# A second level of seven products in the MLP's second layer

## The chip, the cores and the metric

The kernel runs on one core of a Trainium2 chip. The metric is the time of one execution on the device in microseconds. A second number, the span, comes from one execution that the hardware profiler recorded: from its first to its last instruction.

The core has five engines, each with its own queue that it works through in order: TensorE (PE in the profile; loading its stationary operand is listed apart as PEld), VectorE (DVE), ScalarE (ACT), GpSimd (POOL) and SyncE (SP), which here issues nearly all DMA transfers. Matmuls write to PSUM, which has eight banks of 512 fp32 columns; all other operands lie in SBUF; DRAM is reached by DMA.

## The reference

One layer of a diffusion backbone over 256 context tokens and 2048 latent tokens, with a model width of 1024. The part at issue is the MLP at its end:

```
def sq_relu_mlp(h, w1, w2):
    return jnp.square(jax.nn.relu(h @ w1)) @ w2
...
        h = rms_norm(xp, norm2_g[l]) * (1 + sc2) + sh2
        xp = xp + g2 * sq_relu_mlp(h, w1[l], w2[l])
...
        h = rms_norm(xs, norm2_g[l]) * (1 + sc2) + sh2
        xs = xs + g2 * sq_relu_mlp(h, w1[l], w2[l])
```

`w1` is 1024 x 4096, `w2` 4096 x 1024. The second layer multiplies the 2304 x 4096 activations by `w2`, scales by the gate `g2` (one per column, a different one for context and latent tokens), and adds the residual `x`.

## The kernel before

Every fp32 matrix product is done as three fp32r matmuls: each operand is split into a high part (a copy rounded to fp32r, on ScalarE) and a low part (the operand minus its high part, on VectorE, both inputs in SBUF), and `mm3` (lines 86 to 88) issues high x high, low x high or high x low into the same PSUM accumulation.

The stages follow each other: input projection, Fourier mixing and attention (to about 1325 us), output projection and norm, MLP layer one (`w1`, about 1590 to 2273 us), and MLP layer two (`w2`), which the change rewrites. Layer one (lines 1542 to 1544 issue its matmuls) works in 48 steps `q` of seven items `p`; VectorE splits weights there (line 1268) and forms sums of them (line 1514), GpSimd forms sums of its results (`g_add`, lines 1584 to 1590), and `g_stores` (line 1596) writes them to DRAM as `sop[p][b]`, 128 x 16 x 384 each.

Both layers use a scheme of seven products for eight, in the form with 15 additions. For layer two the tokens are halved (`NTH` = 9 tiles of 128 tokens in each half), the 4096 inputs are halved (16 chunks `k` of 128), and the 1024 outputs are halved (512 columns). Each of the seven products is 9 token tiles x 16 chunks x 512 columns, over left operands `sop[p]` (sums of activations, made in layer one) and right operands that are quarters of `w2` or their sums. Three of these sums are made during layer one by `ts_load` and `ts_sum` and put in DRAM as `tsum[k]`; the fourth is a difference of two loads (line 1221).

Layer two runs the products in the order `PO = (1, 2, 6, 7, 5, 3, 4)`. For each product `i` there are three blocks `b` of three token tiles, and for each block 16 chunks `k`; per chunk and tile one `mm3`, 128x128 by 128x512. Three PSUM banks of a block fill side by side; six buffers in all let the next block start while the last is read.

What feeds it:

- `t_load(n)` loads one chunk of the right operand (256 KB) through `raw` (line 1180), a ring of eight; `t_prep(n)` splits it (lines 1223 and 1224) into one of 22 buffers (`OPB` = 9 shared with layer one, `16 + AHEAD - OPB` of its own). A product's 16 chunks stay in SBUF for its three blocks. `PREP` lays down by hand between which matmuls each is split.
- `s_load(m)` loads four chunks of three tiles of the left operand (768 KB, line 1193, a ring of three under the tag `hr`); `s_prep(m)` splits two chunks at a time (128x768, lines 1236 and 1237).
- `y_post` takes a finished product out of PSUM. Running sums `UU` (nine tiles) and `U3` (nine tiles) stay in SBUF for the whole stage. Products 2, 5, 3 and 4 each complete one of the four quarters of the result (`target`): VectorE adds or subtracts the running sum (lines 1765 and 1767), multiplies by the gate (1772) and adds the residual (1773), which `x_load` (line 1748) fetched from `xnew`; `y_store` (line 1779) sends it out.

GpSimd has no work in this stage. Under `manual_schedule` the instructions stand on each engine's queue in exactly the order in which the loops emit them, and SP issues transfers in that order too, waiting where a buffer is not yet free. `mk_gate` forms the gate `g2` during the first product. At the very end the last product's three tiles are finished one after the other so that only one is left after the last matmul (lines 1830 and 1838 to 1844). The first loads and splits of layer two are emitted at the end of layer one (lines 1713 to 1724).

Of the kernel before, what the change touches and what calls it, by code (L numbers as in the profile page):

```python
# [36 lines left out]
def f32(ap):  # L37
    return ap.bitcast(F32)


def body(tc, a, out):
    nc = tc.nc
    ctx = ExitStack()
    with ctx:
# [21 lines left out]
        tsum = [scratch(f"tsum{k}", [P, 3, 512]) for k in range(16)]  # L66
# [1132 lines left out]
        OPB, AHEAD = 9, 6  # L1199
        PO = (1, 2, 6, 7, 5, 3, 4)  # L1200
        w2s = a["w2"][0].rearrange("(n k p) o -> p n k o", p=P, k=16)
        TR, TO, SR, SO, own = {}, {}, {}, {}, {}

        def op(nm, shared=True):
            if shared:
                return [ms2.tile([P, 512], F32R, tag=f"op{x}", name=f"op{x}{nm}", bufs=OPB) for x in "hl"]
            return [own["wk"].tile([P, 512], F32R, tag=f"t{x}", name=f"t{x}{nm}", bufs=16 + AHEAD - OPB) for x in "hl"]

        def t_load(n):

            p, k = PO[n // 16], n % 16
            TR[n] = []
            for rc in {1: (11,), 2: (21,), 3: (22,), 5: (0,), 7: (1,), 6: (2,), 4: (2, 21)}[p]:
                r, c = divmod(rc, 10)
                src = w2s[:, r - 1, k, (c - 1) * 512:c * 512] if r else tsum[k][:, c]
                TR[n].append(raw(f"b{rc}_{n}", src))

        def t_prep(n):
            src, *more = TR.pop(n)
            for t in more:  # L1220
                nc.vector.tensor_sub(src, src, t)
            hi, lo = op(f"T{n}", n % (16 + AHEAD) < OPB)
            nc.scalar.copy(hi, src)
            nc.vector.tensor_sub(lo, src, f32(hi))
            TO[n] = hi, lo

        def s_load(m):
            i, r = divmod(m, 12)
            b, c = divmod(r, 4)
            SR[m] = hr_load(f"sr{m}", sop[PO[i]][b][:, 4 * c:4 * c + 4, :])  # L1230

        def s_prep(m):
            src = SR[m // 2][:, m % 2 * 2:m % 2 * 2 + 2, :]
            pool, bufs = (ms2s, 2) if m % 3 < 2 else (own["t6"], 1)
            hi, lo = (pool.tile([P, 2, 384], F32R, tag=f"s{x}", name=f"s{x}{m}", bufs=bufs) for x in "hl")
            nc.scalar.copy(hi, src)  # L1236
            nc.vector.tensor_sub(lo, src, f32(hi))  # L1237
            SO[m] = hi, lo

# [260 lines left out]
        with c5r, ExitStack() as c5:  # L1502
# [155 lines left out]
            with tc.manual_schedule():  # L1658
                for n, (q, p) in enumerate(ITEMS):
# [42 lines left out]
                    if q - 1 in TSETS and p == 7:  # L1702
                        k = TSETS.index(q - 1)
                        nc.sync.dma_start(tsum[k], TS.pop(k))
# [8 lines left out]
                    if q == NQ - 1 and p == 7:  # L1713
                        s_load(0)
                        for n in range(4):
                            t_load(n)
                        s_load(1)
                    if q == NQ - 1 and p == 4:
                        t_prep(0)
                        s_prep(0)  # L1720
                        for n in (1, 2):
                            t_prep(n)
                squares()
                s_prep(1)
# [7 lines left out]
        with ExitStack() as c6:  # L1732
            wk = own["wk"] = c6.enter_context(tc.tile_pool(name="y_w", bufs=2, reuse_waits="tile"))
            t6 = own["t6"] = c6.enter_context(tc.tile_pool(name="y_t", bufs=2, reuse_waits="tile"))
            pp = c6.enter_context(tc.tile_pool(name="y_p", bufs=2, space=PSUM, reuse_waits="tile"))
            g2 = [wk.tile([P, D], F32, tag=f"g2_{s}", name=f"g2_{s}", bufs=1) for s in range(2)]
            UU, U3, X, ST = {}, {}, {}, []

            def target(p, t):

                return {2: (t, 0), 5: (t + NTH, 1), 3: (t, 1), 4: (t + NTH, 0)}.get(p)

            def x_load(i, b):
                for j in range(3):
                    tg = target(PO[i], 3 * b + j)
                    if tg:
                        X[j] = t6.tile([P, 512], F32, tag="x", name=f"x{i}_{b}_{j}", bufs=4)
# [168 lines left out]
```

## Time and profile before

| | before |
|---|---|
| median of 3 runs | 2979.64 us (2975.64 to 2981.17) |
| span of the profiled execution | 2975.5 us |
| MLP layer two, first to last start of a matmul | 2273.4 to 2970.4 us |
| last 5 us | VectorE on the last tile, its store |
| granted TensorE clock, mean | 0.995 |

Times in rows of the profile are microseconds from the start of the span unless they are marked ns. A row of a group gives the line, engine and operation, the tiles (output, then inputs), the shape, the count, the busy time in us and the mean in ns of one, and then the engine's idle time just before these instructions. A row of a stretch gives, for the interval, its length, then each engine's busy time with its count of instructions in the order PE, PEld, DVE, ACT, POOL, then the granted TensorE clock, the mean share of the 16 DMA engines, and GB/s. A row of single instructions gives start and duration, engine, line, operation, tiles and shape. A matmul's duration overlaps the next one's start, so what it costs is the distance between starts.

### The profile page before, as it was taken

Reading aid. Unit: us, or ns where it says so; the run is one execution under the profiler, and the core shown is the slowest. Engines: PE = TensorE matmul, PEld = TensorE weight load, DVE = VectorE, ACT = ScalarE, POOL = GpSimd, SP = SyncE. Lnnn points to the kernel's source line nnn. Section 1 sums busy time; section 2 is a strip of 40 time slices with the busy share of each in tenths; the row PEclk is TensorE's granted clock in tenths of the full one; section 3 lists DMA queues with packets and bytes.
Section 4 is the critical chain, followed back from the end, with each engine's and each line's share of the span. In section 5 each row is a group of like instructions: output and inputs, shape, how many; then the busy total and the mean of one; then the engine's idle time right before and its main releaser. Section 6 shows DMA issues by size and latency. Waiting matters only on the chain.

```text
span 2975.5 us, 43868 instructions
## 1 busy us (share of the span) xinstructions
PE 2914.6 (98%) x15481; PEld 2512.7 (84%) x15481; DVE 2025.9 (68%) x3379; ACT 1580.1 (53%) x3540; POOL 1022.5 (34%) x839
## 2 busy tenths in 40 slices
PE   8999999999999999999999999999999999999999
PEld 5888887778888888878888999999999888888887
DVE  6666775789888888865458778777776344344554
ACT  4333322688888889964346556556555322232221
POOL 1111112178888988851222333333332000000000
PEclk9999999999999999999999999999999999999999
DMA  7777878512120121215686677676666454445563
GB/s 274 204 195 205 226 195 250 193 52 76 42 110 28 70 84 35 86 58 157 202 251 215 218 239 226 219 238 214 221 200 228 145 171 162 138 145 174 195 215 106
DMA packets 394413, 495.58 MB, mean 167 GB/s; under 512 B 26403, under 2 KB 307056, under 8 KB 391122
## 3 DMA queue, kind: packets, MB, share of 16 engines
q1 hardware_dynamic: 386560, 477.63, 50.4%
q0 software_dynamic: 2992, 7.28, 0.8%
q10 hardware_dynamic: 4642, 7.88, 0.8%
q8 instruction: 122, 2.00, 0.3%
q14 instruction: 97, 0.79, 0.1%
HBM read 315.20 MB, written 179.57 MB: 166 GB/s over the span
## 4 chain that ended last, share of the span: by engine, by line
PE 90%; DVE 3%; ACT 2%; DMA 2%; issue 1%; POOL 1%; SPq 0%; ACTq 0%; DVEq 0%; POOLq 0%
PE Ss L920 10%; PE ps L86 8%; PE ps L87 8%; PE ps L88 8%; PE pj L86 4%; PE pj L88 4%; PE pj L87 4%; PE pts L976 4%; PE po L88 4%; PE po L86 4%; PE po L87 4%; PE pA L1542 2%; PE pA L1543 2%; PE pB L1542 2%; PE pA L1544 2%; PE pC L1544 2%
## 5 line engine op out<-in xcount | busy, mean ns | idle before, releaser
L925 DVE TENSOR_REDUCE mxs<-Ss 128x1 f32<-128x512 f32 x640 | 421.8, 687 | 80.4 <-PE Ss L920 69.9
L1237 DVE TENSOR_TENSOR sl<-sr,sh 128x768 fp32r<-128x768 f32 x168 | 161.7, 963 | 339.9 <-ACT sh L1236 339.4
L967 POOL TENSOR_TENSOR P0s<-P0s,P1s 128x1024 f32<-128x1024 f32 x124 | 365.3, 2946 | 10.3
L1236 ACT CAST sh<-sr 128x768 fp32r<-128x768 f32 x168 | 140.2, 835 | 424.9 <-PE ps L87 424.9
L1584 POOL TENSOR_TENSOR gs<-g,g 128x384 f32<-128x384 f32 x48 | 70.2, 1464 | 483.3 <-ACT g L1554 392.3
L944 ACT ACTIVATE P1s<-Ss,mxs 128x512 f32<-128x512 f32 x320 | 217.3, 694 | 35.6 <-DVE mxs L928 33.4
L86 PE MATMUL pj<-wh,hh 128*128 128x512 f32 x576 | 229.6, 399 | 0.7 <-ACT fo L374 0.7
L87 PE MATMUL ps<-tlT,sh 128*128 128x512 f32 x585 | 229.3, 392 | 0.0
L86 PE MATMUL ps<-thT,sh 128*128 128x512 f32 x585 | 229.2, 392 | 0.0
L87 PE MATMUL pj<-wl,hh 128*128 128x512 f32 x576 | 227.5, 395 | 0.5 <-DVE wl L496 0.5
L88 PE MATMUL ps<-thT,sl 128*128 128x512 f32 x585 | 227.7, 389 | 0.0
L88 PE MATMUL pj<-wh,hl 128*128 128x512 f32 x576 | 226.4, 394 | 0.0
L944 ACT ACTIVATE P0s<-Ss,mxs 128x512 f32<-128x512 f32 x320 | 215.8, 696 | 6.5 <-DVE mxs L928 6.3
L920 PE MATMUL Ss<-KS0s,Qs 128*128 128x512 f32 x640 | 201.8, 424 | 16.9 <-ACT P1s L944 15.6
L920 PE MATMUL Ss<-KS1s,Qs 128*128 128x512 f32 x640 | 210.9, 434 | 4.8 <-ACT P0s L944 4.0
L976 PEld LDWEIGHTS pts<-ident,P0s 128*128 128x128 f32 x1280 | 159.1, 141 | 45.4 <-ACT ahs L982 2.8
L976 PE MATMUL pts<-ident,P0s 128*128 128x128 f32 x1280 | 191.7, 273 | 3.4 <-DVE als L987 1.8
L1553 ACT ACTIVATE g<-uz 128x384 f32<-128x384 f32 x144 | 75.8, 527 | 207.3 <-DVE uz L1576 180.7
L982 ACT CAST ahs<-pts 128x512 fp32r<-128x512 f32 x256 | 151.3, 593 | 47.9 <-PE pts L976 39.7
L987 DVE TENSOR_TENSOR als<-pts,ahs 128x512 fp32r<-128x512 f32 x256 | 165.8, 681 | 11.5 <-ACT ahs L982 11.5
L966 POOL TENSOR_SCALAR P1s<-P1s,tots 128x1024 f32<-128x1024 f32 x124 | 166.8, 1346 | 5.6
L86 PE MATMUL ps<-ophT,sh 128*128 128x512 f32 x423 | 165.9, 392 | 1.1 <-DVE uz L1576 1.1
(615 smaller groups left out, 8248.2 us busy)
## 6 DMA issues: line engine op xcount, KB each, us to landing
sr<-sd SPq DMA_DIRECT2D x84, 768.0 KB, 4.4
a<-in_w SPq DMA_DIRECT2D x184, 256.0 KB, 4.0
sd<-gs SPq DMA_DIRECT2D x192, 192.0 KB, 1.9
sd<-g SPq DMA_DIRECT2D x144, 192.0 KB, 4.0
wm<-in_w_mod SPq DMA_DIRECT2D x32, 512.0 KB, 4.9
Qs<-qd SPq DMA_DIRECT2D x32, 512.0 KB, 3.5
b<-in_w SPq DMA_DIRECT2D x64, 256.0 KB, 4.9
b<-tsum SPq DMA_DIRECT2D x64, 256.0 KB, 4.6
```

The source lines that it names most:

```text
L86: nc.tensor.matmul(ps, lh, rh, start=first, stop=False)
L87: nc.tensor.matmul(ps, lh, rl, start=False, stop=False)
L88: nc.tensor.matmul(ps, ll, rh, start=False, stop=last)
L920: nc.tensor.matmul(S[:, :w], self.Q[:, x, m, j * P:j * P + P], self.hd.KS[m][:, b * 512:b * 512 + w], start=(x == 0), stop=(x == 1))
L925: nc.vector.tensor_reduce(self.mx[j][:, m, b:b + 1], self.S[j, m, b], axis=AX.X, op=ALU.max)
L944: nc.scalar.activation(dst, S, AF.Exp, bias=self.mx[j][:, m, 6:7], accum_out=self.sm[j][:, m, b:b + 1])
L966: nc.gpsimd.tensor_scalar(p, p, tot[:, 3:4], 0.0, op0=ALU.mult, op1=ALU.add)
L967: nc.gpsimd.tensor_add(d, d, p)
L976: nc.tensor.transpose(pt[:, c:c + P], self.p0[j][:, (kb + t) * P:(kb + t + 1) * P], ident)
L982: nc.scalar.copy(t, self.pt[kb])
L987: nc.vector.tensor_sub(t, self.pt[kb], f32(self.A[kb][0]))
L1237: nc.vector.tensor_sub(lo, src, f32(hi))
```

## The change

Layer two is rewritten; layer one keeps its work, except that two of its sums `tsum[k]` now share one DRAM tensor. The order `PO` of the seven outer products stays.

Within each outer product, eight of its nine token tiles are computed with the same scheme once more. The tiles form 2 rows of 4, the 16 chunks form 2 halves of 8, the 512 columns 2 halves of 256. So there are seven inner products `x` in the order 1, 5, 6, 7, 2, 3, 4, of 4 tiles x 8 chunks x 256 columns. The ninth tile is computed directly, in four further pieces (`"p"`) that use right operands which the inner products have anyway, and one extra split (`x = 0`). That gives 32 slots of 24 matmuls of 128x128 by 128x256.

- The left operands of inner products 5, 6, 7 and 3 are sums that GpSimd forms from loaded tiles (`s_sum`, 128x1024); the loads (`r_load`) fetch 8 chunks of one tile, 512 KB in pieces of 512 bytes, and some are fetched twice. ScalarE and VectorE then split each operand of a slot (`s_split`), through a ring of four buffers.
- The right operands are loaded as four quadrants and combined by `t_sum`: for inner products 5 and 6 on VectorE, for 7 and 4 on GpSimd (128x512, two chunks of 256 columns). Each is split (`t_split`) through a ring of 11.
- `v_copy` and `u2_add` take the inner running sums out of PSUM; later inner products accumulate onto banks A, B and C directly. There is one buffer for each of seven banks.
- The outer running sums no longer stay in SBUF. They are DRAM tensors `uu` and `ut`, in nine pieces of 128x512. For each piece of each product `z_load` fetches the sums and the residual, `z_pre` (GpSimd) adds the inner sum, `z_eva` (VectorE, from PSUM) adds the product, `z_mul` (VectorE) multiplies by the gate or stores the sum back to DRAM, `z_out` (GpSimd, and VectorE for the last four pieces) adds the residual and stores the result.
- All of it is put in order by times counted in slots: `at(i, t, fn, ...)` emits an action before slot `t` of product `i`.

The core of the diff:

```diff
-        tsum = [scratch(f"tsum{k}", [P, 3, 512]) for k in range(16)]
+        tsum = [scratch(f"tsum{k}", [P, 2, 3, 512]) for k in range(8)]
+        uu, u3 = ([scratch(f"{x}{n}", [P, 512]) for n in range(9)] for x in ("uu", "ut"))
...
+        TX, SX = (1, 0, 5, 6, 7, 2, 3, 4), (1, 5, 6, 7, 2, 3, 4)
+        QUAD = {"b11": (0, 0), "b12": (0, 1), "b22": (1, 1), "b21": (1, 0)}
...
+        def t_load(i, quad, u):
+            rc, *more = {1: (11,), 2: (21,), 3: (22,), 5: (0,), 7: (1,), 6: (2,), 4: (2, 21)}[PO[i]]
+            nm = f"{quad}_{i}_{u}"
+            if quad in ("b11", "b12"):
+                t = raw(nm, t_src(rc, quad, u))
+            else:
+                t = own["t6"].tile([P, 512], F32, tag="rb", name=nm, bufs=8)
+                nc.sync.dma_start(t.rearrange("p (k f) -> p k f", f=256), t_src(rc, quad, u))
+            TR[i, quad, u] = t
+            for m in more:
+                x = own["t6"].tile([P, 512], F32, tag="rx", name=f"x{nm}", bufs=1)
+                nc.sync.dma_start(x.rearrange("p (k f) -> p k f", f=256), t_src(m, quad, u))
+                nc.vector.tensor_sub(t, t, x)
...
+        def t_split(i, x, u):
+            src = TR[i, {1: "b11", 0: "b12", 5: "b11", 6: "b11", 7: "b12", 2: "b21", 3: "b22", 4: "b11"}[x], u]
+            n = (i * 8 + TX.index(x)) * 4 + u
+            hi, lo = op(f"T{i}_{x}_{u}", n % TRING < OPB)
             nc.scalar.copy(hi, src)
             nc.vector.tensor_sub(lo, src, f32(hi))
...
+            TO[i, x, u] = hi, lo
...
+            last = n % 4 == 3
+            hi, lo = (own["wk" if last else "ys"].tile([P, 1024], F32R, tag=f"s{x}", name=f"so{x}{n}", bufs=1 if last else 3) for x in "hl")
             nc.scalar.copy(hi, src)
             nc.vector.tensor_sub(lo, src, f32(hi))
...
+            SO[key] = [[t[:, k * P:k * P + P] for k in range(8)] for t in (hi, lo)]
...
+            RROLE = {(0, 0): "r0", (0, 1): "r0", (1, 0): "r1", (1, 1): "r2"}
+            def r_load(i, r, c, j, role=None):
+                role = role or RROLE[r, c]
+                t = t6.tile([P, 1024], F32, tag=role, name=f"{role}_{i}_{r}{c}{j}", bufs=4)
+                nc.sync.dma_start(t.rearrange("p (k t) -> p k t", t=P), s_src(i, r, c, j))
+                RQ[i, role, j] = t
...
+            def s_sum(i, x, j):
+                r0, r1, r2 = (RQ.get((i, f"r{n}", j)) for n in range(3))
+                if x == 5:
+                    nc.gpsimd.tensor_add(r1, r1, r2)
+                elif x == 6:
+                    nc.gpsimd.tensor_sub(r1, r1, r0)
+                elif x == 7:
+                    nc.gpsimd.tensor_sub(r2, r0, r2)
+                else:
+                    nc.gpsimd.tensor_sub(r1, r0, r1)
...
+            def t_sum(i, x, u):
+                b11, b12, b22, b21 = (TR.get((i, q, u)) for q in ("b11", "b12", "b22", "b21"))
+                dst, x0, x1, eng = {5: (b11, b12, b11, nc.vector), 6: (b11, b22, b11, nc.vector),
+                                    7: (b12, b22, b12, nc.gpsimd), 4: (b11, b21, b11, nc.gpsimd)}[x]
+                eng.tensor_sub(dst, x0, x1)
...
+            def z_load(i, z):
+                p, n = PO[i], PIECES.index(z)
+                b = BUN[i, z] = flat(f"bun{i}_{n}").rearrange("p (n c) -> p n c", n=3)
+                if p in (2, 6, 7, 3):
+                    nc.sync.dma_start(b[:, 0, :], uu[n])
+                if p in (5, 4):
+                    nc.sync.dma_start(b[:, 0, :], u3[n])
+                if p == 5:
+                    nc.sync.dma_start(b[:, 2, :], uu[n])
+                if target(p):
+                    for t, c, d in spots(p, z):
+                        nc.sync.dma_start(b[:, 1, d], xnew[t][:, c])
...
+            def z_pre(i, z):
+                p, b, (rc, h) = PO[i], BUN[i, z], z
+                if p == 5:
+                    nc.gpsimd.tensor_sub(b[:, 2, :], b[:, 2, :], b[:, 0, :])
+                if p == 1 or rc in (0, 11):
+                    return
+                v = VV["2" if rc == 12 else "1", h]
+                (nc.gpsimd.tensor_sub if p == 4 else nc.gpsimd.tensor_add)(b[:, 0, :], b[:, 0, :], v)
...
+            def z_eva(i, z, bank, step=1):
+                p, t, (rc, h) = PO[i], BUN[i, z][:, 0, :], z
+                ps = BANK[bank, h]
                 if p == 1:
...
+                    if rc in (0, 11):
+                        nc.scalar.copy(t, ps)
+                    else:
+                        nc.vector.tensor_add(t, ps, t if step == 2 else VV["2" if rc == 12 else "1", h])
+                elif p == 4:
+                    nc.vector.tensor_sub(t, t, ps)
+                else:
+                    nc.vector.tensor_add(t, ps, t)
...
+            def z_mul(i, z):
+                p, b = PO[i], BUN[i, z]
+                if p == 5:
+                    nc.vector.tensor_add(b[:, 2, :], b[:, 2, :], b[:, 0, :])
+                    nc.sync.dma_start(uu[PIECES.index(z)], b[:, 2, :])
+                if not target(p):
+                    nc.sync.dma_start((u3 if p == 7 else uu)[PIECES.index(z)], b[:, 0, :])
+                    BUN.pop((i, z))
                     return
...
+                sp = spots(p, z)
+                g = g2[1 if sp[0][0] < 2 else 0][:, sp[0][1]]
+                if len(sp) == 1:
+                    nc.vector.tensor_mul(b[:, 0, :], b[:, 0, :], g)
+                else:
+                    v = b[:, 0, :].rearrange("p (n c) -> p n c", n=2)
+                    nc.vector.tensor_mul(v, v, g.unsqueeze(1).to_broadcast([P, 2, 256]))
...
+            def z_out(i, z):
+                p = PO[i]
+                if not target(p):
                     return
...
+                b = BUN.pop((i, z))
+                (nc.vector if i == 6 and z[0] in (12, 21) else nc.gpsimd).tensor_add(b[:, 0, :], b[:, 0, :], b[:, 1, :])
+                for t, c, d in spots(p, z):
+                    dst = out[0][0][t * P:t * P + P] if t < 2 else out[1][0][t * P - NP:t * P - NP + P]
+                    nc.sync.dma_start(dst[:, c], b[:, 0, d])
...
+            def v_copy(h):
+                if ("1", h) not in VV:
+                    VV["1", h], VV["2", h] = (ms2s.tile([P, 2, 384], F32R, tag=f"s{x}", name=f"v{x}{h}", bufs=2)
+                                              .rearrange("p a b -> p (a b)")[:, 0:512].bitcast(F32) for x in "hl")
+                nc.scalar.copy(VV["1", h], BANK["A", h])
+            def u2_add(h):
+                nc.vector.tensor_add(VV["2", h], BANK["B", h], VV["1", h])
...
+                    at(i, -11 + j, r_load, i, 0, 0, j)
+                    at(i, -8 + j, r_load, i, 1, 0, j)
+                    at(i, -4 + j, r_load, i, 1, 1, j)
+                    if i or j > 1:
+                        at(i, -2.6 + j, split_s, i, 1, j)
+                    elif j:
+                        at(i, -0.6, split_s, i, 1, j)
+                    at(i, 0.4 + j, s_sum, i, 5, j)
+                    at(i, 1.7 + j, r_load, i, 1, 0, j, "r2")
+                    at(i, 4.3 + j, split_s, i, 5, j)
+                    at(i, 4.5 + j, s_sum, i, 6, j)
+                    at(i, 8.3 + j, split_s, i, 6, j)
+                    at(i, 8.5 + j, s_sum, i, 7, j)
+                    at(i, 9.7 + j, r_load, i, 0, 1, j)
+                    at(i, 12.3 + j, split_s, i, 7, j)
+                    at(i, 13.5 + j, s_sum, i, 3, j)
+                    at(i, 14.7 + j, r_load, i, 1, 1, j)
+                    at(i, 16.3 + j, split_s, i, 2, j)
+                    at(i, 22.3 + j, split_s, i, 3, j)
+                    at(i, 26.3 + j, split_s, i, 4, j)
+                    if i:
+                        at(i, -8 + j, t_load, i, "b11", j)
+                        at(i, -4 + j, t_split, i, 1, j)
+                    at(i, -6 + j, t_load, i, "b12", j)
+                    at(i, -2 + j if i else -2, t_load, i, "b22", j)
+                    at(i, 5.7 + j, t_load, i, "b21", j)
+                    at(i, 0.2 + j, t_split, i, 0, j)
+                    at(i, 0.6 + j, t_sum, i, 5, j)
+                    at(i, (2.5, 3.5, 4.2, 5.0)[j], t_split, i, 5, j)
+                    at(i, (4.0, 4.6, 5.2, 5.3)[j], t_sum, i, 6, j)
+                    at(i, 6.2 + j, t_split, i, 6, j)
+                    at(i, 7.8 + j * 0.5, t_sum, i, 7, j)
+                    at(i, 10.2 + j, t_split, i, 7, j)
+                    at(i, 14.2 + j, t_split, i, 2, j)
+                    at(i, 18.2 + j, t_split, i, 3, j)
+                    at(i, 18.5 + j, t_sum, i, 4, j)
+                    at(i, 23.2 + j, t_split, i, 4, j)
...
+                    at(i, 2.7 + 2 * h, v_copy, h)
+                    at(i, 12.6 + 2 * h, u2_add, h)
+                for z, t, bank in (((22, 0), 16, "B"), ((22, 1), 18, "B"), ((11, 0), 20, "A"), ((11, 1), 22, "A"), ((0, 0), 24, "P"),
+                                   ((12, 0), 26, "C"), ((12, 1), 28, "C"), ((21, 0), 30, "B"), ((21, 1), 32, "B")):
+                    end = i == 6 and t == 32
+                    at(i, t - 3, z_load, i, z)
+                    at(i, t - 1, z_pre, i, z)
+                    at(i, t + .55, z_eva, i, z, bank)
+                    if z[0] == 22:
+                        at(i, t + .56, z_eva, i, z, "C", 2)
+                    at(i, t + .6 + (not end) * .4, z_mul, i, z)
+                    at(i, t + .7 + (not end) * 1, z_out, i, z)
...
+            SLOTS = [(1, j) for j in range(4)] + [(1, "p"), (0, "p")] + [(x, j) for x in (5, 6, 7, 2) for j in range(4)] + \
+                    [(2, "p"), (3, "p")] + [(x, j) for x in (3, 4) for j in range(4)]
+            SET = {1: "A", 2: "A", 6: "B", 7: "B", 4: "B", 5: "C", 3: "C"}
...
+                for k in range(8):
+                    th, tl = (t[:, k % 2 * 256:k % 2 * 256 + 256] for t in TO[i, x, k // 2])
+                    nc.tensor.matmul(ps, sh[k], th, start=first and k == 0, stop=False, skip_group_check=True)
+                    nc.tensor.matmul(ps, sh[k], tl, start=False, stop=False, skip_group_check=True)
+                    nc.tensor.matmul(ps, sl[k], th, start=False, stop=last and k == 7, skip_group_check=True)
```

227 lines of the change are left out of this document (97 added, 130 removed).

## Prediction

> **What bounds the kernel now.** I read the shares of the page first, then the busy time of layer two's stretch, then who waits there, then single matmuls.
>
> ```profile
> span 2975.5 us, 43868 instructions
> PE 2914.6 (98%) x15481; PEld 2512.7 (84%) x15481; DVE 2025.9 (68%) x3379; ACT 1580.1 (53%) x3540; POOL 1022.5 (34%) x839
> ...
> L86 PE MATMUL ps<-ophT,sh x423: 387/389/497, 2273.4 to 2969.9; 128*128 128x512 f32 x141
> ...
> L88 PE MATMUL ps<-ophT,sl x423: 388/389/398, 2273.8 to 2970.4; 128*128 128x512 f32 x141
> ...
> 2273.00:2973.00 700.00, 696.70 (x3059) 571.44 (x3058) 330.27 (x434) 206.63 (x294) 5.75 (x4) 1.00 0.50 166
> ...
> ACT sh L1236 <- PE ps L87: 420.4, 146, 3.4
> DVE sl L1237 <- ACT sh L1236: 337.1, 137, 4.1
> ```
>
> The tile rows date the stage: its matmuls start between 2273.4 and 2970.4 us, 697 us. In the row of that stretch (PE, weight load, DVE, ACT, POOL busy, then clock, DMA share and GB/s) PE is busy throughout, DVE 330 of 700 us, ACT 207 and POOL 6. The waits say the same from the other side: ACT stands 420 us until PE has freed an operand buffer, and DVE then stands for ACT. TensorE sets the end here, and everything that feeds it has half its time to spare. That spare time is what the change uses.
>
> **TensorE's part.** Before, a product is 9 tiles x 16 k x 3 matmuls = 432 of 512 columns, in all 3024. After, it is 32 slots (28 of the second level, 4 of the ninth tile) x 8 k x 3 = 768 of 256 columns, in all 5376. What one costs is the distance from start to start, since they are pipelined:
>
> ```profile
> 2499.82 0.39 PE L87 MATMUL ps<-tlT,sh 128*128 128x512 f32 x1
> ...
> 2503.92 0.39 PE L87 MATMUL ps<-oplT,sh 128*128 128x512 f32 x1
> ...
> 901.37 0.28 PE L87 MATMUL po<-als,Vs 128*128 128x256 f32 x1
> ...
> 902.54 0.28 PE L88 MATMUL po<-ahs,Vs 128*128 128x256 f32 x1
> ```
>
> 18 steps of 512 columns take 4.10 us, 0.228 us each. Ten steps of 256, in the attention, take 1.17 us, 0.117 us each, with a fresh weight load each, so no load shows. 5376 x 0.117 = 629 us against 3024 x 0.228 = 689 us. TensorE alone would gain 60 us (an eighth of the work on eight ninths of it, less some fixed time per matmul). One slot is 24 x 0.117 = 2.81 us, a product 90 us.
>
> **What the other engines now do.** Counted over the stage from the order of the built kernel: POOL does 112 additions of 128x1024 (`s_sum`) and 133 of 128x512 (56 `t_sum`, 45 `z_pre`, 32 `z_out`). DVE does 209 low parts of 128x1024, 347 additions or products of 128x512 whose two inputs both lie in SBUF (226 low parts, 56 `t_sum`, 16 differences of loads, 49 in `z_mul` and `z_out`), and 88 that read PSUM. Alone these last:
>
> ```profile
> L967 POOL TENSOR_TENSOR P0s<-P0s,P1s 128x1024 f32<-128x1024 f32 x62 | 148.3, 2392 | 5.2
> ...
> L1422 POOL TENSOR_TENSOR ht<-hTb 128x512 f32<-128x512 f32 x8 | 10.3, 1293 | 0.0
> ...
> L1237 DVE TENSOR_TENSOR sl<-sr,sh 128x768 fp32r<-128x768 f32 x145 | 138.8, 958 | 300.1 <-ACT sh L1236 299.6
> L1224 DVE TENSOR_TENSOR tlT<-b,thT 128x512 fp32r<-128x512 f32 x58 | 39.5, 687 | 14.7 <-ACT thT L1223 14.7
> ...
> L1767 DVE TENSOR_TENSOR c<-ps,uu 128x512 f32<-128x512 f32 x18 | 12.3, 683 | 0.0
> ...
> L1236 ACT CAST sh<-sr 128x768 fp32r<-128x768 f32 x145 | 121.0, 835 | 366.8 <-PE ps L87 366.8
> L1223 ACT CAST thT<-b 128x512 fp32r<-128x512 f32 x58 | 35.4, 618 | 41.2 <-DVE b L1221 31.1 <-PE ps L88 8.6 <-DMA b<-tsum 1.5
> ```
>
> A 1024-wide low part is not there; from 512 to 768 it grows by 0.27 us, so I put 1.23 us. POOL alone: 112 x 2.39 + 133 x 1.29 = 439 us. DVE alone: 209 x 1.23 + 347 x 0.687 + 88 x 0.683 = 257 + 238 + 60 = 555 us. ACT: 226 x 0.62 + 209 x 1.05 (835 plus one more step of 217 ns) + 17 x 0.6 = 370 us. Each is below TensorE's 629, so taken engine by engine all of it is covered and the 60 us would be kept. They do not run side by side, though.
>
> **DVE and POOL exclude each other.** In layer one POOL already adds beside DVE:
>
> ```profile
> 1852.96 0.68 DVE L1514 TENSOR_TENSOR ws<-a,a 128x512 f32<-128x512 f32 x1
> 1856.05 0.56 DVE L1570 TENSOR_TENSOR u<-pB,us 128x384 f32<-128x384 f32 x1 [1.80 <-PE pB L1544]
> 1856.52 1.23 DVE L1268 TENSOR_TENSOR oplW<-ws,ophW 128x512 fp32r<-128x512 f32 x1
> ...
> 1855.20 1.02 POOL L1586 TENSOR_TENSOR gs<-gs,g 128x384 f32<-128x384 f32 x1
> 1856.17 1.03 POOL L1588 TENSOR_TENSOR gs<-g,g 128x384 f32<-128x384 f32 x1
> 1857.15 1.48 POOL L1590 TENSOR_TENSOR gs<-g,gs 128x384 f32<-128x384 f32 x1
> ...
> 1811.83 1.51 DVE L1268 TENSOR_TENSOR oplW<-a,ophW 128x512 fp32r<-128x512 f32 x1
> 1813.26 1.50 DVE L1514 TENSOR_TENSOR ws<-a,a 128x512 f32<-128x512 f32 x1
> 1814.69 1.50 DVE L1268 TENSOR_TENSOR oplW<-ws,ophW 128x512 fp32r<-128x512 f32 x1
> ...
> 1812.87 1.35 POOL L1586 TENSOR_TENSOR gs<-gs,g 128x384 f32<-128x384 f32 x1
> 1814.17 1.47 POOL L1588 TENSOR_TENSOR gs<-g,g 128x384 f32<-128x384 f32 x1
> ```
>
> The addition at 1856.05, one input from PSUM, keeps its 0.56 us beside POOL. The low part at 1856.52, both inputs from SBUF, takes 1.23 instead of 0.68: it ends 0.55 us after POOL's addition ended at 1857.20. POOL's next one then takes 1.48 instead of 1.02 and ends 0.88 us after DVE's end at 1857.75. From 1811.83 on both have a queue, and they take turns: DVE 512 and POOL 384 together advance by 1.43 us a pair, against 0.68 + 1.02 = 1.70 alone. So one turn costs its duration alone less half of the 0.27 us in which the ends overlap, 0.14 us.
>
> Put on the stage's counts: POOL 112 x 2.25 + 133 x 1.15 = 405 us; DVE's two-input work 209 x 1.09 + 347 x 0.547 = 418 us. Together 823 us of one resource, against 629 us of matmuls. Bounds of the unknown price, that of a 1024-wide turn: were only what grows with width exclusive (POOL 1.10 us per 512 from the 1024 and 512 rows, DVE 0.54 from the 768 and 512), it is 112 x 2.20 + 133 x 1.10 + 209 x 1.08 + 347 x 0.54 = 805; with nothing overlapped and DVE's PSUM work behind it in the same queue, 439 + 555 = 994. I take the turn-taking value, because those rows have both queues full, as they will be here.
>
> The Trainium skill, "SBUF — State Buffer", section "Who interferes with whom", states that a VectorE instruction with two SBUF inputs and a GpSimd one that reads SBUF lock each other out for the whole instruction. Taken to the letter the sum would be 439 + 495 = 934 us in place of 823; the pairs above show 0.27 us less each.
>
> The load is uneven. Slots 0 to 16 of a product hold all 16 `s_sum`, four `t_sum` of POOL, eight of DVE, and some 17 + 18 low parts: 36 + 5 + 4 + 19 + 10 = 74 us for 48 us of matmuls. In slots 17 to 31 stand 13 + 14 low parts and 4 `t_sum` (27 us), seven `z_pre` (8 us, not in product 1) and nine `z_mul` and `z_out` (15 us, only where the product goes to the output): products 1, 6 and 7 ask 27, 35 and 35 us of a stretch in which the matmuls take 42. There TensorE sets the pace, and 15 + 7 + 7 = 29 us are added: 852 us. Buffers let POOL run ahead four sums at most (`r1` has four), which gives some of it back; handing over (POOL, then ACT's copy of 1.05 us, then DVE, each in a fixed order) costs some again. I put 880 us, 7% above 823, in the lower half between 805 and 994.
>
> **The rest of the change.** DMA: 184 loads of 512 KB, 128 of 256 KB for the weights, 63 of 256 KB for the partial results, 36 for x, 36 partial and 36 output stores: 175 MB. Issues on SP's queue: 184 + 128 + 63 + 68 + 36 + 68 = 547 (x and output in pieces of 256 columns, but for the ninth tile).
>
> ```profile
> q1 hardware_dynamic: 110073, 112.44, 68.9%
> ...
> 1807.81 2.14 SPq L1180 DMA_DIRECT2D a<-in_w  x4
> ...
> 1841.16 3.83 SPq L1596 DMA_DIRECT2D sd<-gs  x4
> ```
>
> The first row is layer one's from 1700 to 2200 us, 112 MB at 69% of the 16 engines, in packets of about 1 KB; so 175 MB take 175 / 112 x 500 x 0.69 = 539 us of the engines, 61% of 880 us. The new `r` loads come in 512-byte pieces as `a` does, 0.54 us an issue; between this and the 0.96 us of `sd<-gs`, waits included, 547 issues take 295 to 525 us. Neither is a bound. What stands behind a waiting store on SP are loads 8 to 11 slots (23 to 31 us) ahead of their use; that lead is their cover, and I cost them at nothing, up to 63 x 1 us if it is used up. The tail is one 0.69 us step longer than now, the head the same. PSUM sets are single, but each is read 8 or more slots before it is written again, except the copy of B behind `u2_add` with two slots (5.6 us): a DVE that is late by more stops TensorE there too, and this is the same lateness, already in the sum.
>
> **The rivals.** (1) The turns don't matter: the additions find gaps and the matmuls set the end. For it speaks that every engine alone has room (555 and 439 against 629); against it the pairs at 1811 us. Stage 629 + 8 (what the present one has over its 689) = 637 us: 2975.5 - 60 + 4 = 2920 us in the median. It would hold if the two-input work of DVE and POOL took under 629 us together. Chance 0.07. (2) TensorE's clock falls with the gaps as well:
>
> ```profile
> 1300.00:1320.00 20.00, 18.16 (x134) 16.99 (x134) 11.88 (x23) 8.77 (x22) 2.31 (x6) 0.94 0.03 8
> 1320.00:1340.00 20.00, 16.72 (x88) 13.68 (x88) 10.63 (x17) 8.16 (x18) 4.14 (x8) 0.83 0.49 171
> 1360.00:1380.00 20.00, 19.44 (x98) 16.25 (x99) 9.47 (x13) 9.14 (x22) 6.88 (x6) 1.00 0.75 225
> ```
>
> With PE idle for 3.3 of 20 us the granted clock was 0.83, with 0.6 us 1.00. At 0.83 the matmuls take 629 / 0.83 = 758 us, still below 823, so the loss shows in the second halves alone: 7 x 42 x 0.2 = 60 us at most, and with late hand-overs it comes to 940 to 1000 us, 3225 to 3285. Against it: the gaps should be about 1 us a slot, not one long one. Chance 0.2. The Trainium skill, "TensorE: Matmul & The Clock Gate", section "Part 1: The HAM clock gate", has the clock halved after an idle window of some 3.4 us and nothing between; by it short gaps cost nothing, and a stage wholly at half clock would be 1258 us, which no row here suggests. (3) Turn-taking holds, but POOL and DVE run so far ahead in the light stretches that little but part of the heavy ones shows: first halves 7 x (74 - 48) = 182 us over 629, no more than half hidden, 720 to 780 us, 3000 to 3060. Chance 0.1.
>
> **How the numbers follow.** Forecast: 2975.5 + (880 - 697) = 3158.5 in the profile's terms, and the median of the runs stands 4.1 us over the profiled span: 3163 us. Its own range goes from 805 us of stage (the lower bound, 3088) to 942 (3225); chance 0.61. With (2) and the upper half of (3) taken in: 3030 to 3285. Left out are (1), the rest of (3), and 0.02 for within 0.2% (6 us, what a measurement can tell here). So slower 0.91, the same 0.02, faster 0.07.
>
> **What would show it.** In the stage DVE's 1024-wide low parts last clearly over 1.23 us (near 2) and its 512-wide ones over 0.69, POOL's 1024-wide sums near 3 us instead of 2.39, while DVE's additions from PSUM keep 0.68. TensorE's matmuls stay 0.117 us apart inside a slot and wait between slots for low parts from DVE, most in the first half of each product; product 5 is the longest, 1 the shortest. ACT no longer waits for PE but for POOL and DVE. It is wrong if DVE's low parts keep their durations beside POOL, or if SP's queue or the clock (below 0.9 over the stage) is what TensorE waits for.

## The result and the profile after

The changed kernel takes 3240.41 us (median of 4 runs, 3237.41 to 3241.99) against 2978.89 us before: 1.088 times as long, with a 95% interval of 1.0866 to 1.0896. The forecast was 3163 us and a range of 3030 to 3285; the measured time lies in that range, above the 3088 to 3225 us that the forecast's own sum gave. The profiled execution spans 3240.1 us. Its page begins:

```profile
span 3240.1 us, 49867 instructions
PE 2957.2 (91%) x17833; PEld 2657.3 (82%) x17833; DVE 2516.8 (78%) x3589; ACT 1718.2 (53%) x3703; POOL 1623.3 (50%) x1084
```

Layer two runs from 2273.4 us to the last start of a matmul at 3234.3 us: 961 us instead of 697. Cut into the seven products (from the first matmul on bank A to the next product's), the view of stretches reads (length; busy time of PE, PEld, DVE, ACT, POOL with counts; clock; DMA share; GB/s):

```profile
2273.40:2419.80 146.40, 109.32 (x802) 105.72 (x802) 112.59 (x86) 57.58 (x80) 68.45 (x30) 0.86 0.69 192
2419.80:2540.40 120.60, 99.89 (x771) 96.75 (x770) 112.90 (x88) 46.66 (x61) 83.81 (x33) 0.94 0.61 176
2540.40:2670.20 129.80, 102.85 (x770) 100.10 (x769) 112.24 (x87) 49.00 (x65) 83.97 (x34) 0.91 0.66 190
2670.20:2794.00 123.80, 101.85 (x770) 99.80 (x770) 108.64 (x85) 50.27 (x67) 77.77 (x30) 0.90 0.65 187
2794.00:2927.80 133.80, 106.01 (x770) 103.31 (x769) 124.30 (x95) 47.19 (x62) 99.97 (x42) 0.90 0.65 195
2927.80:3094.20 166.40, 113.14 (x770) 108.90 (x769) 125.66 (x102) 51.00 (x67) 98.58 (x44) 0.85 0.67 195
3094.20:3234.40 140.20, 104.21 (x770) 100.57 (x768) 122.25 (x102) 43.48 (x56) 93.11 (x37) 0.88 0.44 131
```

A product of 90 us of matmuls takes 121 to 166 us, and DVE and POOL together are busy for longer than each stretch lasts: their busy time holds waiting for each other. The groups of the stage show that:

```profile
L1266 DVE TENSOR_TENSOR sol<-r,soh 128x1024 fp32r<-128x1024 f32 x194 | 373.6, 1927 | 42.1 <-ACT soh L1265 41.0 <-DMA ut<-bun 1.0
L1241 DVE TENSOR_TENSOR oplT<-b,ophT 128x512 fp32r<-128x512 f32 x182 | 236.0, 1299 | 26.2 <-ACT ophT L1240 26.2
L1785 POOL TENSOR_TENSOR r<-r,r 128x1024 f32<-128x1024 f32 x28 | 76.2, 2739 | 65.8 <-DMA uu<-bun 38.2 <-DMA r<-sd 26.7 <-DVE oplT L1241 0.7
L1787 POOL TENSOR_TENSOR r<-r,r 128x1024 f32<-128x1024 f32 x28 | 112.0, 4021 | 52.4 <-DVE sol L1266 52.4
L1789 POOL TENSOR_TENSOR r<-r,r 128x1024 f32<-128x1024 f32 x28 | 86.5, 3108 | 0.0
L1791 POOL TENSOR_TENSOR r<-r,r 128x1024 f32<-128x1024 f32 x28 | 86.1, 3096 | 0.0
...
L1855 DVE TENSOR_TENSOR bun<-bB,bun x20: 676/678/692, 2493.4 to 3107.7; 128x512 f32<-128x512 f32 x20
```

The 1024-wide low parts last 1.93 us where they should need 1.23, the 512-wide ones 1.30 instead of 0.69, and POOL's sums 2.7 to 4.0 in the mean of their lines instead of 2.39. The additions with one input from PSUM keep their 0.68 us. In the order of time, from the slots of inner products 6 and 7 in the fourth product:

```profile
2723.09 2.86 DVE L1241 TENSOR_TENSOR oplT<-b,ophT 128x512 fp32r<-128x512 f32 x1
2725.87 3.40 DVE L1266 TENSOR_TENSOR sol<-r,soh 128x1024 fp32r<-128x1024 f32 x1
2729.20 0.68 DVE L1891 TENSOR_TENSOR vl<-bB,vh 128x512 f32<-128x512 f32 x1
...
2722.05 9.46 POOL L1789 TENSOR_TENSOR r<-r,r 128x1024 f32<-128x1024 f32 x3
```

From 2723.09 to 2725.87 one 512-wide turn of DVE and one sum of POOL go by: 2.78 us, by the prediction's prices 0.55 + 2.25 = 2.80. From there to 2729.20, 3.33 us, by its prices 1.09 + 2.25 = 3.34. The price of a wide turn, which no row of before had shown, was right in this pair.

Where TensorE waits is told by its own waits (total us, times, longest):

```profile
PE bB L1977 <- DVE sol L1266: 64.7, 36, 5.6
PE bP L1977 <- DVE sol L1266: 35.4, 9, 9.3
PE bC L1977 <- DVE sol L1266: 31.5, 11, 10.8
PE bB L1975 <- DVE vl L1891: 36.8, 14, 3.9
PE bA L1975 <- ACT soh L1265: 15.2, 1, 15.2
```

Most are for a low part. The 36.8 us are for the copy of bank B behind `u2_add`, which stands in VectorE's queue between the low parts. The eight slots on bank B of inner products 6 and 7 (22.6 us of matmuls) last 41.3 to 43.9 us in every one of the seven products, and in the fourth POOL is busy, working or shut out, for all of them:

```profile
2707.90:2749.30 41.40, 28.30 (x195) 27.06 (x193) 39.56 (x18) 14.52 (x19) 41.40 (x17) 0.88 0.36 102
```

Eight of the 21 blocks of four slots behind them, in the last 14 slots of the products, last 11.2 to 11.4 us from first to last start, which is 2.8 us a slot: there TensorE goes at full pace. The others last longer.

### The profile page after: what moved, and what is told of

Read it like the earlier page. It is cut to its first block, busy times and chain, and to the rows that moved or that the text cites. A ratio compares the mean times of both kernels' runs of the same rounds, so it can differ in the third digit from the quotient of the medians.

```text
span 3240.1 us, 49867 instructions
## 1 busy us (share of the span) xinstructions
PE 2957.2 (91%) x17833; PEld 2657.3 (82%) x17833; DVE 2516.8 (78%) x3589; ACT 1718.2 (53%) x3703; POOL 1623.3 (50%) x1084
## 4 chain that ended last, share of the span: by engine, by line
PE 59%; issue 11%; POOL 10%; DVE 9%; DMA 7%; ACT 2%; SPq 1%; DVEq 0%; POOLq 0%; ACTq 0%
PE Ss L921 9%; PE pj L87 4%; PE pj L89 4%; PE pj L88 4%; PE pts L977 4%; PE po L89 4%; PE po L87 4%; PE po L88 4%; DVE sol L1266 3%; POOL r L1787 2%; DVE oplT L1241 2%; POOL b L1806 2%; PE pA L1568 1%; PE pA L1570 1%; PE pA L1569 1%
## 5 line engine op out<-in xcount | busy, mean ns | idle before, releaser
L1266 DVE TENSOR_TENSOR sol<-r,soh 128x1024 fp32r<-128x1024 f32 x194 | 373.6, 1927 | 42.1 <-ACT soh L1265 41.0
L1265 ACT CAST soh<-r 128x1024 fp32r<-128x1024 f32 x194 | 202.8, 1047 | 332.6 <-PE bB L1976 122.5
L1241 DVE TENSOR_TENSOR oplT<-b,ophT 128x512 fp32r<-128x512 f32 x184 | 237.3, 1293 | 26.2 <-ACT ophT L1240 26.2
L1977 PE MATMUL bB<-ophT,sol 128*128 128x256 f32 x592 | 185.4, 313 | 52.8 <-DVE sol L1266 52.8
L1975 PE MATMUL bB<-ophT,soh 128*128 128x256 f32 x592 | 183.2, 309 | 34.8 <-DVE vl L1891 34.8
L1240 ACT CAST ophT<-b 128x512 fp32r<-128x512 f32 x184 | 112.7, 616 | 176.2 <-DVE b L1806 73.2
L1976 PE MATMUL bB<-oplT,soh 128*128 128x256 f32 x592 | 181.6, 307 | 1.1 <-DVE oplT L1241 1.1
L1977 PEld LDWEIGHTS bB<-ophT,sol 128*128 128x128 f32 x592 | 128.1, 216 | 59.6 <-DVE sol L1266 59.4
```

What stands on the lines that cost most here:

```text
L1977: nc.tensor.matmul(ps, sl[k], th, start=False, stop=last and k == 7, skip_group_check=True)
```

## The experiments

Experiments for which no interval is given ran once; the four runs of the changed kernel lie within 5 us of each other. The first four ask whether exclusion costs the time, or GpSimd's being late, or something else. "Shared work" below means the sum of turns of DVE and POOL, 823 us in the changed kernel.

**The sums left out.**

```diff
             def s_sum(i, x, j):
+                return
```

> Left out: the 112 sums of left operands on GpSimd (the raw tiles are split and multiplied instead). Theory (DVE's two-input work and POOL's additions exclude each other): the shared work falls from 823 to 571 us, below the 629 us of matmuls; layer two takes 660 to 740 us instead of 961, the run 2940 to 3020 us. Rival (loads, SP's queue, the clock or the fixed order hold TensorE up): over 850 us in layer two, over 3130 us.

Measured: 3030.8 us (kernel before beside it 2977.2). The time falls by 210 us, which the rival excludes; it ends 11 us above the theory's range.

**The sums replaced by memsets.**

```diff
-                if x == 5:
-                    nc.gpsimd.tensor_add(r1, r1, r2)
...
+                for _ in range(2):
+                    nc.gpsimd.memset(r2 if x == 7 else r1, 0.5)
```

> Each of the 112 sums on GpSimd is replaced by two memsets of the same tile, so GpSimd is about as busy at the same places and the splits still wait for it, but it reads nothing. Left out: the sums' values. Theory (exclusion while GpSimd reads): DVE's 1024-wide low parts fall from 1.93 to about 1.3 us and layer two to 670 to 760 us, the run to 2950 to 3040 us. Rival (GpSimd's own lateness in the chain of sum, copy and low part is what costs): low parts may be short, but TensorE waits as before, 3180 to 3240 us.

Measured: 3021.1 us. GpSimd's queue still carries something before each split, and yet 219 us are gone. The stretches of the seven products in this run, second to fourth and sixth:

```profile
2391.70:2484.80 93.10, 91.65 (x770) 91.24 (x769) 85.51 (x87) 47.02 (x61) 54.07 (x42) 1.00 0.79 228
2484.80:2581.00 96.20, 93.25 (x770) 92.85 (x769) 78.46 (x87) 49.14 (x65) 59.55 (x50) 0.98 0.89 255
2581.00:2672.30 91.30, 91.30 (x771) 91.30 (x771) 77.52 (x84) 49.86 (x66) 54.03 (x46) 1.00 0.87 252
...
2775.60:2907.70 132.10, 104.00 (x770) 101.33 (x769) 95.50 (x104) 50.86 (x67) 74.02 (x60) 0.88 0.85 249
```

Three products now run at 91 to 96 us, with TensorE at 1.00 or close to it. The sixth still takes 132.

The run has a weakness: two memsets take 1.91 us, a real sum alone 2.39. So one with three:

> As the run with memsets, but three for each sum: two took 1.91 us where a sum alone takes 2.39, three should take 2.87. Left out: the sums' values. Theory (only reading excludes): GpSimd is busier than with real sums and the run still ends at 3010 to 3060 us. Rival (GpSimd's duration in the chain costs): clearly later than the run with two memsets, 3100 us or more.

Measured: 3080.6 us, between the two. GpSimd's memsets took 0.95 us each, so 107 us more of them cost 59 us, although DVE's wide low parts were no longer than before (1352 ns in the mean against 1452). So both expectations missed: a sum's own duration counts too, in the chain of sum, copy and low part. Three memsets (2.87 us) last longer than a sum alone (2.39), so at least the 160 us between 3081 and the changed kernel's 3240 are due to reading. Put in proportion for 2.39 us, a sum that reads nothing would give some 3050 us and 190 us for reading (worked out, not run; leaving the sums out gave 3031, no less than two memsets, so the cost is not in proportion throughout). Reading is the larger part, being late the smaller.

**All of GpSimd's work replaced by memsets.** `t_sum` of products 7 and 4, `z_pre` and `z_out` as well:

```diff
-                eng.tensor_sub(dst, x0, x1)
+                if eng is nc.gpsimd:
+                    for _ in range(2):
+                        eng.memset(dst, 0.5)
+                else:
+                    eng.tensor_sub(dst, x0, x1)
...
```

> As the run with two memsets for each sum, and GpSimd's other work (differences of right operands, work on results) also replaced by two memsets each. Left out: these values. Theory: no exclusion is left, VectorE's low parts last 1.23 and 0.69 us, and what stays above 629 us of matmuls is the start (some 30 us) and the waits for the differences (some 30 us): layer two 685 to 715 us, the run 2965 to 2995 us. Rival (something else as large is hidden): 3010 us or more.

Measured: 2997.3 us, 2 us above the range. The low parts are back at their own durations, though GpSimd is busy for 348 of 715 us:

```profile
L1266 DVE TENSOR_TENSOR sol<-r,soh 128x1024 fp32r<-128x1024 f32 x194 | 236.8, 1222 | 60.7 <-ACT soh L1265 60.3
L1241 DVE TENSOR_TENSOR oplT<-b,ophT 128x512 fp32r<-128x512 f32 x183 | 124.9, 686 | 30.2 <-ACT ophT L1240 29.9
```

The Trainium skill, "SBUF — State Buffer", section "Who interferes with whom", states that VectorE's two-input work contends with a GpSimd instruction that reads SBUF and not with one that only writes it; 1222 and 686 ns beside 490 memsets of GpSimd agree.

Layer two still takes 714 us. From the starts of its products (2275.2, 2394.9, 2765.1, 2887.1 and the end at 2989.7 among them) the first lasts 120 us, the sixth 122, the seventh 103, against 91 for the second to fourth: 29 + 31 + 12 us, with 5 in the fifth 77 in all. GpSimd's reading has no part in that rest; whether the memsets' own time has was not tried.

**The same load put on the kernel before.** This asks whether turns cost time as such, or only when their sum passes that of the matmuls. GpSimd adds each new high part to a spare tile, once or twice:

```diff
                                     s_prep(m + 2)
+                                    for _ in range(1):
+                                        nc.gpsimd.tensor_add(spare, spare, f32(SO[m + 2][0]))
```

> The kernel before, with one addition of 128x768 on GpSimd beside each split of a left operand in layer two (166, reading the new high part; results go to a spare tile). Theory (turns cost only when the two engines' sum is over the matmuls' time): 166 x 1.70 = 282 us of GpSimd and some 244 us of two-input work on VectorE make 526 us, under 689: the low parts get longer, the run stays at 2970 to 2995 us. Rival (each low part that waits delays TensorE): 3030 us or more.

> As the run before, with two additions beside each split (332). GpSimd alone needs 332 x 1.84 = 611 us, which would fit under 689; with VectorE's turns it is 564 + 244 = 808 us. Theory: layer two 800 to 850 us, the run 3080 to 3135 us. Rival (no exclusion, each engine fits by itself): 2970 to 3000 us.

Measured: with one, 2994.1 us, ratio 1.0054 (1.0031 to 1.0077); with two, 3116.0 us. DVE's 512-wide low parts, of one and of two:

```profile
L1224 DVE TENSOR_TENSOR tlT<-b,thT 128x512 fp32r<-128x512 f32 x65 | 89.7, 1388 | 13.9 <-ACT thT L1223 11.8 <-DMA b<-tsum 1.1 <-DMA b<-in_w 1.1
```

```profile
L1224 DVE TENSOR_TENSOR tlT<-b,thT 128x512 fp32r<-128x512 f32 x65 | 123.5, 1908 | 9.2 <-ACT thT L1223 9.2
L1813 POOL TENSOR_TENSOR spare<-spare,sh 128x768 f32<-128x768 f32 x332 | 751.9, 2265 | 72.8 <-ACT sh L1236 48.3
```

With one addition the low part already lasts twice as long, and the run is only half a per cent longer: TensorE is fed in time, since 526 us of turns fit beside 689. With two, where either engine alone would still fit, layer two takes 838 us (2271.5 to 3109.4) against 808 worked out. Both expectations held, the first at the upper end of its range (2970 to 2995 us).

**The sums on VectorE.** First the 112 of `s_sum`, then the 56 of `t_sum` as well:

```diff
-                    nc.gpsimd.tensor_add(r1, r1, r2)
+                    nc.vector.tensor_add(r1, r1, r2)
...
```

> The 112 sums of left operands move from GpSimd to VectorE; nothing is left out. Theory: 112 turns of 2.25 us become 112 of 1.09, the shared work falls from 823 to 693 us; layer two 720 to 790 us, the run 3000 to 3070 us. Rival (VectorE is the engine that is short of time, whoever holds the port): it gets 112 x 1.23 = 138 us more to do and the run goes above 3240 us.

> As the run before, and the 56 differences of right operands move to VectorE too; GpSimd keeps only the work on results. Theory: the shared work is 418 + 122 + 31 + 89 = 660 us; layer two 690 to 760 us, the run 2970 to 3040 us. Rival (VectorE short of time): slower than the run before by 56 x 0.69 = 38 us or more.

Measured: 3136.3 and 3108.1 us, 66 and 68 us above the ranges. More work on the busiest engine made the kernel 104 and 132 us faster, which is the theory's sign and not its rivals'. Both missed by nearly the 77 us that the run without any reading showed outside the turns, and which their sums left out; that it is the same time was not shown. The block of inner products 6 and 7 fell from between 41 and 44 us to between 24 and 28 us in both.

**The work on results on VectorE,** `z_pre` and `z_out`:

```diff
-                (nc.gpsimd.tensor_sub if p == 4 else nc.gpsimd.tensor_add)(b[:, 0, :], b[:, 0, :], v)
+                (nc.vector.tensor_sub if p == 4 else nc.vector.tensor_add)(b[:, 0, :], b[:, 0, :], v)
...
```

> The changed kernel with the work on results (additions before and after the gate, 77 of 128x512) on VectorE instead of GpSimd; nothing left out. Theory: 77 turns of 1.15 us become 77 of 0.55, the shared work 823 to 777 us, the run 3180 to 3210 us. Rival (VectorE is short of time, not the port): 77 x 0.69 = 53 us longer, 3260 us or more.

Measured: 3249.6 us. The theory missed, and so did the rival: the run is 9 us longer. By the prices the shared work fell by 46 us over the stage, but, as far as the blocks show, not where TensorE was waiting for it: the block of inner products 6 and 7 lasts 41.7 to 47.2 us, no less than in the changed kernel. Besides, DVE now waits in its own queue for the partial results:

```profile
L1842 DVE TENSOR_TENSOR bun<-bun,vh 128x512 f32<-128x512 f32 x24 | 27.2, 1134 | 17.6 <-DMA bun<-uu 12.9 <-DMA b<-tsum 4.6
```

**Product 4's right operands.** The sixth product, in which these are fetched, is the longest, and DVE's waits there name a load:

```profile
DVE b L1234 <- DMA xb<-in_w: 29.1, 9, 10.1
```

First more buffers (`bufs=1` to `bufs=3` for tag `rx`):

> The changed kernel with three buffers in place of one for the second load of product 4's right operands (tag rx); nothing left out. Theory (beside the exclusion, VectorE stands in line behind differences that wait for these loads one at a time, 46 us in all): product index 5 falls from 166 to about 135 us, the run to 3200 to 3225 us. Rival (these waits are idle time that the port would take anyway): 3235 to 3245 us.

Measured: 3236.6 us, ratio to before 1.0872 (1.084 to 1.0903). The rival held: no gain that the runs tell apart. In that run DVE still waits 40.5 us for these loads over the stage, of 46.0 in the changed kernel. The reason stands in the code: `t_load` emits the difference right behind the load, so DVE reaches it while the load is on its way, however many buffers there are. So the difference was moved, with the three buffers kept:

```diff
-                nc.vector.tensor_sub(t, t, x)
+                XR[i, quad, u] = x
...
+                    if i == 6:
+                        for quad, t0 in (("b11", -8), ("b12", -6), ("b22", -2), ("b21", 5.7)):
+                            at(i, t0 + j + 2.2, t_diff, i, quad, j)
```

> The changed kernel with the 16 differences of product 4's right operands put 2.2 slots behind their loads in VectorE's queue, instead of right behind them, and three buffers for the second load; nothing left out. Theory (VectorE, which works in order, stands still until such a load has landed, 40 us in all, buffers or not): the run falls by 20 to 40 us to 3200 to 3220 us. Rival (idle time that costs nothing): 3230 to 3242 us.

Measured: 3218.5 us, 1.0809 (1.0777 to 1.084): 22 us less than the changed kernel and within the range.

**The gains together.** Sums on VectorE, differences later, and for the start:

```diff
                         s_ahead(1)
+                        s_ahead(2)
...
-                    at(i, -11 + j, r_load, i, 0, 0, j)
+                    at(i, -11 + j if i else (-3.5 + j if j < 3 else -11), r_load, i, 0, 0, j)
```

> All sums on VectorE, the differences 2.2 slots later, and at the start a third left operand fetched during layer one and the loads put in order of use; nothing left out. Theory: the run with all sums on VectorE (3108 us) less 20 to 40 us for the differences and 5 to 15 us for the start: 3055 to 3085 us. Still above the kernel before, since the shared work (660 us) is over the matmuls' 629. Rival (gains hide each other): 3090 us or more.

Measured: 3088.3 us, 1.0371 (1.0341 to 1.0402): 20 us less than with all sums on VectorE, 3 us above the theory's range and 2 below the rival's. It is the best complete form found and still 111 us slower than the kernel before. From first to last start the first four slots fall from 30.5 to 24.4 us, but the next ones wait instead: the first 18 slots of layer two take 86.7 us (2275.4 to 2362.1) against 87.1 (2273.6 to 2360.8). So the start gained nothing.

## Why the prediction was right, and where it was off

- **The range** held because the interval of rival (2), the falling clock, had been taken in: 3240 lies in that rival's 3225 to 3285 us and above the forecast's own range. That the direction and the cause were right is no luck. That the time fell inside the range is partly so, since it had been widened for a mechanism that explains at most 33 of the 81 us missing from the sum (see the clock, below).
- **TensorE's part** was right where the clock was full: 24 matmuls of 256 columns go by in 2.8 us, as the attention's rows said, and the run without any reading has whole products at 91 us for 90 worked out.
- **The turns** were right in kind and in price (2.78 and 3.33 us for 2.80 and 3.34). Taking all reading from GpSimd brings 243 us back (3240 to 2997), some of it because memsets are shorter than sums. That TensorE alone would have won 60 us (seven products of 91 us against the 697 of before) and that DVE and POOL have room one by one is true, and decides nothing.
- **The stage's sum of 823 us** is a floor, not the measure; that is the first step that was off. The halves were the better view, though rougher than it looks. First halves (17 slots) were put at 74 us. In order, the products take 106.5, 73.6, 86.4, 79.1, 76.7, 88.9 and 94.7 us for their first 18 slots: three are near the price, the first, third, sixth and seventh are not. Moving 46 us of work that lay in the second halves gained nothing.
- **"The head the same"** failed. The first 18 slots take 106.5 us, 32 more than the price of a first half, and 29 us of it stay in the run without reading. Who waits in the first stretch, and SP's issues there:

```profile
POOL r L1785 <- DMA r<-sd: 26.5, 3, 24.0
PEld bA L1975 <- ACT soh L1265: 15.5, 1, 15.5
...
ACT soh L1265 <- DMA r<-sd: 12.8, 1, 12.8
...
2281.82 8.15 SPq L1775 DMA_DIRECT2D r<-sd  x6
```

  SP issues the loads of left operands behind layer one's last stores, from 2281.8 us, 8 us after layer two's first matmul, and the first slots and sums wait for them.
- **The 16 differences of product 4** were counted as turns of 0.55 us, 9 us in all. Their price is that DVE waits for a DMA in front of everything behind them: 22 us by the run that moved them. The prediction asked what queues behind a waiting store on SP and not what queues behind a waiting difference on DVE. Product 5, forecast as the longest, took 134 us; the sixth, which fetches for product 4, 166. Product 1, forecast as the shortest, took 146 with its late start, the second longest.
- **Sizes.** 880 us were put for 961. Of the 81 missing, the start is put at 32 and the differences at 22; the remaining 27 are not assigned by a run. Being late, the chain of sum, copy and low part, is a candidate: the memset runs show that it has a price. The starts and ends of single instructions in the trace give a second account, worked out and tested by no run. An instruction of the shared work is running for 853 of the 961 us, so the 823 were counted nearly right. For 108 us none is: 36 in the last 14 slots of products 1, 6 and 7, where 29 were forecast, 20 in the first 18 slots of the stage, 28 in the last 14 of the sixth product, and 24 elsewhere.
- **ACT's waits.** The forecast had ACT no longer wait for PE. For the copies of left operands it still does, more than for POOL; the ring of four buffers makes it wait until TensorE is done with one:

```profile
ACT soh L1265 <- PE bB L1976: 122.5, 40, 9.8
ACT soh L1265 <- POOL r L1787: 35.2, 12, 7.1
```

- **The clock.** It fell to 0.89 over the stage, below the 0.9 named as a sign against the forecast, but it fell with TensorE's waits: without GpSimd's reading it is 0.96. Two stretches of the first product, its first 18 slots and its last 14:

```profile
2273.40:2379.90 106.50, 69.42 (x466) 65.82 (x466) 82.23 (x53) 36.87 (x53) 65.58 (x28) 0.81 0.59 163
2379.90:2419.80 39.90, 39.90 (x339) 39.90 (x338) 30.35 (x34) 20.70 (x27) 2.88 (x2) 1.00 0.95 271
```

  0.81 stands where operands were missing, 1.00 where they were there, 2.85 us a slot. Another sign failed here: matmuls were to stay 0.117 us apart inside a slot. Behind a wait the trace has stretches at about half that pace (0.21 us):

```profile
2719.29 0.58 PE L1977 MATMUL bB<-thT,sol 128*128 128x256 f32 x1 [3.01 <-DVE sol L1266]
2719.67 0.41 PE L1975 MATMUL bB<-thT,soh 128*128 128x256 f32 x1
2719.89 0.41 PE L1976 MATMUL bB<-tlT,soh 128*128 128x256 f32 x1
2720.10 0.41 PE L1977 MATMUL bB<-thT,sol 128*128 128x256 f32 x1
```

  Counted over the stage, 749 of 5375 steps lie between 0.16 and 0.26 us, and at 0.12 us they would take 70 us less. 36 of these lie in the first 18 slots of the second to sixth products. There an instruction of the shared work is running for 401 of 405 us, so the shared work sets the pace and a faster TensorE would only have waited longer. The other 33 us may have lengthened the stage; that is the most that the clock adds by this count, and no run separates it.
- **SP's queue** waits 17 to 39 us in a product for a buffer that POOL's sum frees (`r` loads behind line 1789). That these waits cost nothing was argued from their lead and was not tried by itself.

## What to carry to other kernels

Before work is given to GpSimd beside VectorE, add up on one account the time of GpSimd's instructions that read SBUF and of VectorE's with two SBUF inputs, and set that against the engine that ends last, for each stretch between two points where queues can even out. Room on each engine alone says nothing: 526 us on that account beside 689 of matmuls cost half a per cent, 808 cost 4.6%. And an operation that waits for a DMA belongs in an in-order queue as late as its user allows; more buffers alone gained nothing that the runs tell apart.

## What was not expected of the hardware

The granted clock fell in every heavy stretch, though the waits are spread over it. I had held against that rival that the gaps would be short. In the first 18 slots of the fourth product TensorE was busy 60 of 79 us, its longest wait for an operand was 6.2 us and the others 3 us or less, and the clock was 0.87:

```profile
2670.20:2749.30 79.10, 59.85 (x435) 58.40 (x434) 71.92 (x47) 31.34 (x43) 68.25 (x24) 0.87 0.52 151
...
PE bB L1977 <- DVE sol L1266: 9.2, 4, 3.0
PE bP L1977 <- DVE sol L1266: 6.2, 1, 6.2
PE bB L1975 <- DVE vl L1891: 3.9, 2, 2.5
```

The trace's record of the granted clock has only two values in this stage, full and half, in pieces of 3.4 us and multiples of it. In this stretch the half pieces begin at 2684.0, 2718.1 and 2735.2 us, and in the 3.4 us before each TensorE was idle for 1.9 to 2.0 us, by its starts and modelled ends. So pieces in which TensorE was idle for somewhat more than half were followed by half ones here; a gap as long as a whole piece was not needed.

And sums of one size under one load differ by place: those of inner product 6 (line 1787), which wait until VectorE has read the operand they overwrite, show 4.0 us, the others 2.7 to 3.1. Why was not looked into.
